# Scaling tokens by two weights: from contiguous 4 MB groups to 128 consecutive tokens in each partition

## The chip, the cores and the metric

The kernel runs on one core of one Trainium2 chip; the other cores run nothing. The metric is the device time of one execution in microseconds. Three executions of the kernel before took 239.26, 242.16 and 251.51 us; their median, 242.16 us, is the time before.

## The reference

The input x has 16 x 1024 tokens of 512 float32 values. Each token has k = 2 expert weights, and the output holds the token once for each weight, multiplied by it. The expert indices are an input, but the result doesn't use them.

```python
batch, seq, hidden, n_experts = 16, 1024, 512, 8          # k = 2
x_expanded = x[:, :, np.newaxis, :].repeat(k, axis=2)
weights = expert_weights[..., np.newaxis]
return (x_expanded * weights).astype(np.float32)          # [16, 1024, 2, 512]
```

So 33.5 MB of x and 0.13 MB of weights are read and 67.1 MB are written, with one multiplication for each number written.

## The kernel before

The 16,384 tokens are cut into eight groups of 2048 consecutive tokens. A group is one tile of 128 partitions, and a partition holds T = 16 tokens of it. For this the helper `rows(flat, done, T)` takes rows done*128 to (done+T)*128 of a flat array, which are one contiguous block, and gives the first 16 to partition 0, the next 16 to partition 1 and so on. In HBM the row that one partition reads (16 tokens of 2 KB, 32 KB) therefore starts 32 KB behind the one of its neighbour, and the row that it writes (64 KB) starts 64 KB behind.

A slot is a tile of 128 x 64 KB, and there are three slots. The load of a group (L120, issued from ScalarE's queue) puts the 32 KB of x into the upper half of the slot. The products are then written from the bottom of the slot upwards, over x that has already been used: VectorE does tokens 0 to 7, 8 to 11, 12 to 13 and 14 in four instructions (L136), and ScalarE does the two products of token 15 in two (L153). SyncE's queue then stores the 64 KB rows (L178). In the first and the last group the first eight tokens are stored by themselves (L174) as soon as their product is done, so these groups have two stores of half the size. The load of group i + 2 is issued behind the last products of group i, from ScalarE's queue, and waits until the store that empties its slot has landed. All instructions stand in the order in which the program writes them.

The weights: a partition of a group needs the 32 weights of its 16 tokens, and the whole tile `w_tile` holds 128 partitions x 8 groups x 32 weights. In HBM the weights of one group's partition are only 128 bytes in a row. The kernel therefore loads them as 128 rows of 1 KB (`weights_in`, L68, from SyncE's queue), in which partition q has the weights of 128 consecutive tokens, and sorts them on the chip (`weights_spread`): eight transposes on TensorE (L84) against an identity that GpSimd writes (L55 and L56), two copies on VectorE (L89), eight transposes back (L95) and a last copy into `w_tile` (L100). The order at the start is: load of the weights, loads of groups 0, 1 and 2, sorting, and then the loop over the groups.

Of the kernel before, what the change touches and what calls it, by code (L numbers as in the profile page):

```python
# [1 line left out]

# [4 lines left out]


@with_exitstack
def kernel(  # L10
    ctx: ExitStack,
    tc: tile.TileContext,
    x: bass.AP,
    expert_indices: bass.AP,
    expert_weights: bass.AP,
    out: bass.AP,
):
    nc = tc.nc

    batch, seq, hidden = x.shape  # L20
    k = expert_weights.shape[-1]
    P = nc.NUM_PARTITIONS
    ntok = batch * seq
    assert ntok % P == 0

    f32 = mybir.dt.float32
    row = k * hidden


    groups = [16] * 8  # L30
    assert sum(groups) * P == ntok
    TX = max(groups)

    xf = x.rearrange("b s h -> (b s) h")
    of = out.rearrange("b s k h -> (b s) (k h)")
    wf = expert_weights.rearrange("b s k -> (b s) k")

    w_pool = ctx.enter_context(tc.tile_pool(name="w_pool", bufs=1))
    slots = ctx.enter_context(tc.tile_pool(name="slots", bufs=3))
    raw_pool = ctx.enter_context(tc.tile_pool(name="raw_pool", bufs=1))  # L40
    psum = ctx.enter_context(
        tc.tile_pool(name="psum", bufs=2, space=bass.MemoryType.PSUM)
    )

    w_tile = w_pool.tile([P, sum(groups) * k], f32)

    def rows(flat, done, T):
        return flat[done * P : (done + T) * P, :].rearrange("(p a) n -> p (a n)", a=T)

    B = 8
    M = P // B
    ident = w_pool.tile([P, P], f32)
    nc.gpsimd.memset(ident, 0.0)  # L55
    nc.gpsimd.affine_select(  # L56
        out=ident,
        in_=ident,
        compare_op=mybir.AluOpType.not_equal,
        fill=1.0,  # L60
        base=0,
        pattern=[[-1, P]],
        channel_multiplier=1,
    )

    def weights_in(head, G, T):
        raw_tile = raw_pool.tile([G * M, B * T * k], f32, name=f"raw{T}_tile")
        nc.sync.dma_start(  # L68
            out=raw_tile,
            in_=wf[head * P : (head + G * T) * P, :].rearrange(  # L70
                "(q a) n -> q (a n)", a=B * T
            ),
        )
        return raw_tile

    def weights_spread(raw_tile, head, G, T):
        n = T * k
        col_tile = raw_pool.tile([n, G * P], f32, name=f"col{T}_tile")
        cols = col_tile.rearrange("c (q r) -> c q r", r=B)
        step = 4  # L80
        for r0 in range(0, B, step):
            up_tile = psum.tile([n, step, G * M], f32)
            for r in range(step):
                nc.tensor.transpose(  # L84
                    up_tile[:, r, :],
                    raw_tile[:, (r0 + r) * n : (r0 + r + 1) * n],
                    ident[: G * M, : G * M],
                )
            nc.vector.tensor_copy(  # L89
                out=cols[:, :, r0 : r0 + step],  # L90
                in_=up_tile.rearrange("c r q -> c q r"),
            )
        down_tile = psum.tile([P, G * n], f32)
        for g in range(G):
            nc.tensor.transpose(  # L95
                down_tile[:, g * n : (g + 1) * n],
                col_tile[:, g * P : (g + 1) * P],
                ident[:n, :n],
            )
        nc.vector.tensor_copy(  # L100
            out=w_tile[:, head * k : (head + G * T) * k], in_=down_tile
        )

    ctx.enter_context(tc.manual_schedule())

    starts = [sum(groups[:i]) for i in range(len(groups))]
    loaded = []

    def load(i):
        if i >= len(groups):
            return
        T = groups[i]
        slot_tile = slots.tile([P, TX * row], f32)
        loaded.append(slot_tile)
        src = rows(xf, starts[i], T)
        at = T * (row - hidden)
        nc.scalar.dma_start(out=slot_tile[:, at : at + T * hidden], in_=src)  # L120


    def ranges(T):
        lo, out = 0, []
        while lo < T - 1:
            hi = lo + 1
            while (hi + 1) * k <= T * (k - 1) + lo and hi < T - 1:
                hi += 1
            out.append((lo, hi))
            lo = hi  # L130
        return out

    def products(slot_tile, T, lo, hi, w_at):
        m = hi - lo
        at = T * (row - hidden) + lo * hidden
        nc.vector.tensor_tensor(  # L136
            out=slot_tile[:, lo * row : hi * row].rearrange(
                "p (t k h) -> p t k h", t=m, k=k
            ),
            in0=slot_tile[:, at : at + m * hidden]  # L140
            .rearrange("p (t h) -> p t h", t=m)
            .unsqueeze(2)
            .to_broadcast([P, m, k, hidden]),
            in1=w_tile[:, w_at + lo * k : w_at + hi * k]
            .rearrange("p (t k) -> p t k", t=m)
            .unsqueeze(3)
            .to_broadcast([P, m, k, hidden]),
            op=mybir.AluOpType.mult,
        )

    def last(slot_tile, T, w_at):
        for c in range(T * k - k, T * k):
            nc.scalar.mul(  # L153
                out=slot_tile[:, c * hidden : (c + 1) * hidden],
                in_=slot_tile[:, T * row - hidden : T * row],
                mul=w_tile[:, w_at + c : w_at + c + 1],
            )

    raw_tile = weights_in(0, 8, 16)
    load(0)  # L160
    load(1)
    load(2)
    weights_spread(raw_tile, 0, 8, 16)

    for i, T in enumerate(groups):
        slot_tile = loaded[i]
        outr = rows(of, starts[i], T)
        w_at = starts[i] * k
        done = 0
        for lo, hi in ranges(T):  # L170
            products(slot_tile, T, lo, hi, w_at)
            if i in (0, len(groups) - 1) and done == 0:
                done = hi
                nc.sync.dma_start(  # L174
                    out=outr[:, : done * row], in_=slot_tile[:, : done * row]
                )
        last(slot_tile, T, w_at)
        nc.sync.dma_start(  # L178
            out=outr[:, done * row :], in_=slot_tile[:, done * row : T * row]
        )  # L180
        if i:
            load(i + 2)

# [1 line left out]
_INS = ['x', 'expert_indices', 'expert_weights']  # L185
_OUTS = [((16, 1024, 2, 512), 'float32')]


# [23 lines left out]
```

## Time and profile before

| | before |
|---|---|
| median of three runs | 242.16 us (239.26 to 251.51) |
| the profiled execution's own time | 239.3 us |
| its span, from the first to the last instruction | 237.5 us |
| bytes moved | 100.80 MB, of which 33.69 MB read and 67.11 MB written |
| mean rate over the span | 424 GB/s |
| busy: VectorE | 134.7 us (57%) |
| busy: ScalarE | 12.8 us (5%) |
| busy: TensorE | 2.9 us (1%) |
| DMA packets | 2736 |

A single execution is profiled; its own time is longer than the span by 1.8 us, which lie outside the first and the last recorded instruction. It is close to the fastest of the three runs. The DMA share is the mean over the core's 16 DMA engines, and packets are counted when they end, so that a short stretch can show more or less than was moved in it. Queue q1 is the one that SyncE issues on (stores and weights), q10 that of ScalarE (loads of x).

### The profile page before, as it was taken

The page shows a single profiled execution, that of the slowest core. Times are in us where ns is not written, and L with a number is a line of the kernel's source. Part 1 is how long each engine was busy: PE and PEld are TensorE (multiplying, and loading weights), DVE is VectorE, ACT ScalarE, POOL GpSimd, SP SyncE. Part 2 cuts the span into 40 slices and gives each one's busy share as a digit, 9 for nine tenths or more (in the row PEclk, how much of TensorE's full clock was granted, in tenths as well). Part 3 has the DMA queues.
Part 4 walks back from the last instruction along what each step waited for, and adds up shares of the span by engine and source line. Part 5 has one row for each costly group of instructions (what it writes and reads, how often), then busy time and mean ns, then how long its engine had stood idle before and what let it go on. Part 6 is the DMA issues. An engine that isn't in the chain of part 4 may idle for free.

```text
span 237.5 us, 184 instructions
## 1 busy us (share of the span) xinstructions
PE 2.9 (1%) x16; PEld 1.9 (1%) x16; DVE 134.7 (57%) x35; ACT 12.8 (5%) x17; POOL 0.7 (0%) x6
## 2 busy tenths in 40 slices
PE   0400000000000000000000000000000000000000
PEld 0300000000000000000000000000000000000000
DVE  0289999999600089900998009970199602995000
ACT  0020020110200000020001100020000200002000
POOL 1000000000000000000000000000000000000000
DMA  7999999999899899899799898998998989989996
GB/s 284 444 441 441 353 441 441 436 447 441 375 419 530 353 441 530 353 441 530 337 458 430 370 524 353 441 530 353 441 530 348 447 386 453 486 353 441 441 441 265
DMA packets 2736, 100.80 MB, mean 424 GB/s; under 512 B 304, under 2 KB 432, under 8 KB 432
## 3 DMA queue, kind: packets, MB, share of 16 engines
q1 hardware_dynamic: 1584, 67.24, 65.5%
q10 hardware_dynamic: 1152, 33.55, 33.2%
HBM read 33.69 MB, written 67.11 MB: 424 GB/s over the span
## 4 chain that ended last, share of the span: by engine, by line
DMA 61%; DVE 28%; ACT 2%; issue 0%; DVEq 0%; ACTq 0%
DMA slot_tile<-in_x_dram 33%; DMA out_dram<-slot_tile 29%; DVE slot_tile L136 28%; ACT slot_tile L153 2%; DVEq L136 0%; ACTq L120 0%
## 5 line engine op out<-in xcount | busy, mean ns | idle before, releaser
L136 DVE TENSOR_TENSOR slot_tile<-slot_tile,w_tile 128x8192 f32<-128x8192 f32 (+3 forms) x32 | 132.9, 4158 | 71.6 <-DMA slot_tile<-in_x_dram 70.7
L153 ACT ACTIVATE slot_tile<-slot_tile,w_tile 128x512 f32<-128x512 f32 x16 | 11.5, 721 | 192.5 <-DVE slot_tile L136 192.3
L89 DVE COPY col_tile<-up_tile 32x512 f32<-32x512 f32 x2 | 1.4, 678 | 9.6 <-PE up_tile L84 9.6
L153 ACT ACT_TABLE_LOAD x1 | 1.3, 1283 | 13.2 <-DMA slot_tile<-in_x_dram 13.2
L84 PE MATMUL up_tile<-ident,raw_tile 128*32 128x128 f32 x8 | 1.9, 411 | 8.4 <-DMA raw_tile<-in_expert_weights_dram 8.4
L84 PEld LDWEIGHTS up_tile<-ident,raw_tile 128*32 128x32 f32 x8 | 1.0, 135 | 8.8 <-issue 8.4
L100 DVE COPY w_tile<-down_tile 128x256 f32<-128x256 f32 x1 | 0.4, 424 | 1.1 <-PE down_tile L95 1.1
L95 PE MATMUL down_tile<-ident,col_tile 32*128 32x32 f32 x8 | 1.1, 292 | 0.8 <-DVE col_tile L89 0.8
L95 PEld LDWEIGHTS down_tile<-ident,col_tile 32*128 32x128 f32 x8 | 0.9, 214 | 1.3 <-DVE col_tile L89 1.3
L56 POOL TENSOR_SCALAR_AFFINE_SELECT ident<-ident 128x128 f32<-128x128 f32 x1 | 0.3, 292 | 0.1
L55 POOL MEMSET ident<- 128x128 f32 x1 | 0.2, 204 | 0.3 <-POOLq L196 0.3
L196 POOL MEMSET const-bfloat16-1.0<- 128x1 bf16 x1 | 0.1, 101 | 0.0
L196 POOL MEMSET const-uint8-127<- 128x1 uint8 x1 | 0.1, 101 | 0.0
L196 POOL MEMSET const-float32-0.0<- 128x1 f32 x1 | 0.1, 98 | 0.2 <-issue 0.2
L196 POOL MEMSET const-float32-1.0<- 128x1 f32 x1 | 0.1, 98 | 0.0
## 6 DMA issues: line engine op xcount, KB each, us to landing
slot_tile<-in_x_dram ACTq DMA_DIRECT2D x8, 4096.0 KB, 32.6
out_dram<-slot_tile SPq DMA_DIRECT2D x4, 4096.0 KB, 19.5
raw_tile<-in_expert_weights_dram SPq DMA_DIRECT2D x1, 128.0 KB, 7.5
out_dram<-slot_tile SPq DMA_DIRECT2D x6, 35.9
```

The lines of the kernel that those rows point to most:

```text
L55: nc.gpsimd.memset(ident, 0.0)
L56: nc.gpsimd.affine_select(out=ident, in_=ident, compare_op=mybir.AluOpType.not_equal, fill=1.0, base=0, pattern=[[-1, P]], channel_multipl ...
L84: nc.tensor.transpose(up_tile[:, r, :], raw_tile[:, (r0 + r) * n : (r0 + r + 1) * n], ident[: G * M, : G * M],)
L89: nc.vector.tensor_copy(out=cols[:, :, r0 : r0 + step], in_=up_tile.rearrange("c r q -> c q r"),)
L95: nc.tensor.transpose(down_tile[:, g * n : (g + 1) * n], col_tile[:, g * P : (g + 1) * P], ident[:n, :n],)
L100: nc.vector.tensor_copy(out=w_tile[:, head * k : (head + G * T) * k], in_=down_tile)
L136: nc.vector.tensor_tensor(out=slot_tile[:, lo * row : hi * row].rearrange("p (t k h) -> p t k h", t=m, k=k), in0=slot_tile[:, at : at + m ...
L153: nc.scalar.mul(out=slot_tile[:, c * hidden : (c + 1) * hidden], in_=slot_tile[:, T * row - hidden : T * row], mul=w_tile[:, w_at + c : w_ ...
L196: nc = _bacc.Bacc("TRN2", target_bir_lowering=False, num_devices=1)
```

## The change

The helper `rows` no longer takes a contiguous block. It gives each partition 128 consecutive tokens of the whole array, and a group is 16 of these tokens in each partition: group 0 has tokens 0 to 15 of every partition's 128, group 1 tokens 16 to 31, and so on. Rows are as long as before (32 KB read, 64 KB written), but the start of one partition's row now lies 256 KB behind that of its neighbour in x, and 512 KB behind in the output. With this the weights of a partition are 128 consecutive pairs, 1 KB, for all groups together, so that one load of 1 KB rows fills `w_tile` as it is used. The identity, the transposes, the copies and the two pools for them go. The loop, the products, the slots and the order of the loads and stores stay.

```diff
-    raw_pool = ctx.enter_context(tc.tile_pool(name="raw_pool", bufs=1))
-    psum = ctx.enter_context(
-        tc.tile_pool(name="psum", bufs=2, space=bass.MemoryType.PSUM)
-    )
...
     def rows(flat, done, T):
-        return flat[done * P : (done + T) * P, :].rearrange("(p a) n -> p (a n)", a=T)
...
-    ident = w_pool.tile([P, P], f32)
-    nc.gpsimd.memset(ident, 0.0)
-    nc.gpsimd.affine_select(
...
-    def weights_in(head, G, T):
...
-    def weights_spread(raw_tile, head, G, T):
...
+        return flat.rearrange("(p a) n -> p a n", p=P)[:, done : done + T, :].rearrange(
+            "p a n -> p (a n)"
         )
...
-    raw_tile = weights_in(0, 8, 16)
-    load(0)
-    load(1)
-    load(2)
-    weights_spread(raw_tile, 0, 8, 16)
+    nc.sync.dma_start(out=w_tile, in_=rows(wf, 0, ntok // P))
+    for i in range(3):
+        load(i)
```

More of the change, by code (lines that the diff above doesn't have):

```diff
@@ L39 @@
     slots = ctx.enter_context(tc.tile_pool(name="slots", bufs=3))
-    raw_pool = ctx.enter_context(tc.tile_pool(name="raw_pool", bufs=1))
-    psum = ctx.enter_context(
-        tc.tile_pool(name="psum", bufs=2, space=bass.MemoryType.PSUM)
-    )
     w_tile = w_pool.tile([P, sum(groups) * k], f32)
     def rows(flat, done, T):
-        return flat[done * P : (done + T) * P, :].rearrange("(p a) n -> p (a n)", a=T)
-    B = 8
-    M = P // B
-    ident = w_pool.tile([P, P], f32)
-    nc.gpsimd.memset(ident, 0.0)
-    nc.gpsimd.affine_select(
[L57 to L64, printed above, removed]
-    def weights_in(head, G, T):
[L67 to L74, printed above, removed]
-    def weights_spread(raw_tile, head, G, T):
[L77 to L101, printed above, removed]
+        return flat.rearrange("(p a) n -> p a n", p=P)[:, done : done + T, :].rearrange(
+            "p a n -> p (a n)"
         )
```

## The prediction

> **What bounds the kernel now.** I read the page's table of engines first, then the DMA rows, then the rate in stretches, then the start in order of time, and last the chain. The first lines of the page:
>
> ```profile
> PE 2.9 (1%) x16; PEld 1.9 (1%) x16; DVE 134.7 (57%) x35; ACT 12.8 (5%) x17; POOL 0.7 (0%) x6
> ...
> DMA  7999999999899899899799898998998989989996
> GB/s 284 444 441 441 353 441 441 436 447 441 375 419 530 353 441 530 353 441 530 337 458 430 370 524 353 441 530 353 441 530 348 447 386 453 486 353 441 441 441 265
> DMA packets 2736, 100.80 MB, mean 424 GB/s; under 512 B 304, under 2 KB 432, under 8 KB 432
> ...
> q1 hardware_dynamic: 1584, 67.24, 65.5%
> q10 hardware_dynamic: 1152, 33.55, 33.2%
> ```
>
> No compute engine is near full: VectorE, the busiest, works 57% of the span. The DMA row is at 8 or 9 tenths in every slice but three. The two queues' packets take 65.5 + 33.2 = 98.7% of what 16 DMA engines have in the span, so the DMA engines stand idle for 1.3% of 237.5 us, 3.1 us in all. The single slices swing between 337 and 530 GB/s because packets of 32 and 64 KB are counted when they end; longer stretches are steadier. Two answers by stretch (columns: the stretch, its length, busy time and count of PE, PEld, DVE, ACT and POOL, the TensorE clock, the DMA share, GB/s):
>
> ```profile
> 0.00:13.00 13.00, 2.92 (x16) 1.93 (x16) 1.78 (x3) 0.00 (x0) 0.70 (x6) 1.00 0.92 373
> 13.00:22.00 9.00, 0.00 (x0) 0.00 (x0) 8.76 (x2) 1.28 (x1) 0.00 (x0) 1.00 0.94 408
> 22.00:49.00 27.00, 0.00 (x0) 0.00 (x0) 26.83 (x8) 2.89 (x4) 0.00 (x0) 1.00 1.02 427
> 49.00:201.00 152.00, 0.00 (x0) 0.00 (x0) 81.40 (x21) 7.21 (x10) 0.00 (x0) 1.00 1.00 435
> ```
>
> ```profile
> 3.00:12.00 9.00, 2.83 (x16) 1.93 (x16) 1.36 (x2) 0.00 (x0) 0.00 (x0) 1.00 0.96 413
> 48.00:80.00 32.00, 0.00 (x0) 0.00 (x0) 15.13 (x4) 1.54 (x3) 0.00 (x0) 1.00 1.01 436
> ...
> 200.00:209.00 9.00, 0.00 (x0) 0.00 (x0) 8.69 (x1) 0.00 (x0) 0.00 (x0) 1.00 0.81 350
> 209.00:236.00 27.00, 0.00 (x0) 0.00 (x0) 7.95 (x3) 1.44 (x2) 0.00 (x0) 1.00 0.99 427
> ```
>
> From 49 to 201 us, when loads and stores run together, the DMA engines are full (share 1.00) and move 435 GB/s. What idle time there is lies at the start (8% of 13 us is 1.0 us, 6% of the next 9 us is 0.5 us) and near the end (19% of the 9 us from 200 is 1.7 us), together 3.2 us, as the queues' shares said. The last hole has a cause that the chain of waits shows:
>
> ```profile
> 167.53 32.62 DMA slot_tile<-in_x_dram
> ...
> 200.28 8.70 DVE slot_tile L136
> ```
>
> The last load lands at about 200.2 us, and until its first product is done 8.70 us later only the rest of the store before it is left to move. So the kernel is a full stream of packets with 3 us of holes; its time is bytes divided by the rate of a packet, plus these holes.
>
> **The change part by part.** *The sorting of the weights goes.* It is 16 matmuls with their weight loads, three VectorE copies and two GpSimd instructions. The start in order of time (start, length, engine, line):
>
> ```profile
> 0.74 0.37 SPq L68 DMA_DIRECT2D raw_tile<-in_expert_weights_dram  x1
> ...
> 8.40 1.86 PE L84 MATMUL up_tile<-ident,raw_tile 128*32 128x128 f32 x8 [8.40 <-DMA raw_tile<-in_expert_weights_dram]
> 9.45 0.68 DVE L89 COPY col_tile<-up_tile 32x512 f32<-32x512 f32 x1 [9.45 <-PE up_tile L84]
> ...
> 12.12 0.42 DVE L100 COPY w_tile<-down_tile 128x256 f32<-128x256 f32 x1 [1.15 <-PE down_tile L95]
> 13.18 1.28 ACT L153 ACT_TABLE_LOAD   x1 [13.18 <-DMA slot_tile<-in_x_dram]
> 13.21 8.69 DVE L136 TENSOR_TENSOR slot_tile<-slot_tile,w_tile 128x8192 f32<-128x8192 f32 x1 [0.66 <-DMA slot_tile<-in_x_dram]
> ```
>
> The weights are in place at 12.12 + 0.42 = 12.54 us. The first product begins at 13.21 us, and what released it is the load of group 0, which lands at 13.1 us. So the sorting lies wholly under that load, 0.66 us short of it, and its removal is worth 0 on the path. The 1.78 us of VectorE copies and 2.92 us of TensorE lie in the same stretch; nothing waits for them. What becomes late next is nothing: the product still waits for group 0.
>
> *The load of the weights* has the same shape as before, 128 rows of 1 KB from the same contiguous 128 KB, issued first on SyncE's queue, at 0.74 us. It only has another target. It lands about 7.5 us after its issue:
>
> ```profile
> raw_tile<-in_expert_weights_dram SPq DMA_DIRECT2D x1, 128.0 KB, 7.5
> ```
>
> ```profile
> 21.93 0.34 SPq L174 DMA_DIRECT2D out_dram<-slot_tile  x1
> ```
>
> So `w_tile` will be ready at about 8.3 us, with 4.9 us to spare against group 0. If that cover went, the first product would be late by the excess; behind it on VectorE stand all products, and behind those the first store at 21.93 us. It would take a landing at 18 us, 10 us after the one seen, to cost 4.9 us. Cost: 0, with 0 at both ends.
>
> *Order and queues.* The listing of the changed program has the same ten stores behind one weight load on SyncE's queue, the same eight loads between the same products on ScalarE's, and the same 32 products on VectorE. No queue gains a wait. The GpSimd instructions that go (0.7 us, with constants that stay) have nobody behind them.
>
> *The pitch of the rows.* All 100.80 MB move in packets of the same length: 1024 of 32 KB for the loads, 768 of 64 KB and 512 of 32 KB for the stores, 128 of 1 KB for the weights, and small ones. What changes is where they lie: the streams that the 16 DMA engines run side by side start 256 KB (reads) and 512 KB (writes) apart for each partition instead of 32 and 64 KB, so eight times as far. The trace of before shows no such pitch, and its cost is the whole question, since the packets fill 98.7% of the span. The nearest rows are those of one kind alone. From 3 to 12 us only loads run, at 32 KB: 413 GB/s at a share of 0.96, so 430 at full share. From 209 to 236 us only stores run, at 64 KB: 427 / 0.99 = 431. One doubling of the pitch (and the change from reading to writing) costs nothing to be seen, which gives the end at 0 cost. For the other end there is no row of a long pitch; the furthest that these same transfers have been seen to slow is the slowest of the three runs, 251.51 us against the profiled execution's 239.3, so +12.2 us, which is 5% of the packets' time. An end below nothing: the best long stretch, 48 to 80 us, had 436 GB/s. At that rate 100.80 MB take 231.2 us; with the 3.1 us of holes, which nothing here removes, 234.3, that is 3.2 us under the span. So the pitch costs between -3.2 and +12.2 us.
>
> I take a third of the upper end, +4.1 us. This is a choice: the row at zero is the nearest, but it stands for one doubling of the pitch, and three are made here, in both directions. It is nearer to zero than to the slow run, as the only row that does speak of pitch asks.
>
> The Trainium skill speaks against this change, in "DMA: Bandwidth & Descriptors", section "Latency and other measured facts": copies of 128 rows of 16 KiB between HBM tensors fell to 207 GB/s a direction where the rows' pitch was 512 KiB and to 164 at 2 MiB, while a padded pitch gave 214. By an estimate from that page the stores' packets (65.5% of the span, 155.6 us) would take 214/207 as long, 5.3 us more, so 244.6 us; with the loads at the same rate it would be 7.9 us and 247.2. No run here has shown it yet.
>
> **The sum.** 239.3 (the profiled execution) + 0 (sorting) + 0 (weights' load) + 0 (order) + 4.1 (pitch) = 243.4 us. The profiled execution is 2.9 us faster than the median of the runs shown, so this is 1.7% over the former and 0.5% over the latter. A difference under 2% (4.8 us) is about what can't be told from no change in this kernel.
>
> **The rivals.**
>
> *The pitch costs over 2%.* Mechanism: the 16 DMA engines take rows of equal length side by side, in step; if starts that are a large power of two apart meet in the same part of the memory, each packet waits for others. It decides from 4.8 us, which is a packet rate of 435 x 234.4 / 239.2 = 426 GB/s or less in the stretch from 49 to 201 us. For it: nothing in the span could hide a slower packet, as the share is 1.00 there. Against it: the pitch of before is a power of two as well, and loads alone and stores alone reach the same rate with it. Its price lies between 4.8 and the 12.2 us of the upper end; the middle, 8.5, gives 247.8 us. The Trainium skill's row above is a rule of this kind.
>
> *The new pitch is better.* Streams that lie further apart may disturb each other less, when loads and stores mix. For it: the mixed stretch is 435 at share 1.00, and single stretches differ by some GB/s. Against it: loads alone, stores alone and the mixture all give 430 to 436 at full share, which looks like the DMA engines' own limit and leaves nothing for the memory to give. Price: up to -3.2, so 236.1 us.
>
> *The change does more than it says at the start*, that is, the path begins with the sorting after all and the product starts once the weights are there, at 8.3 us. That would be worth up to 13.21 - 8.3 = 4.9 us, so 234.4 us. Against it stands the row at 13.21 with its releaser: the load of group 0 is needed whatever the weights do. And an earlier product would still meet a DMA that is 94 to 102% busy from 13 to 49 us.
>
> **How the numbers follow.** The forecast (within 2%, 243.4 us, pitch costs little) gets 0.50. The slow pitch gets 0.40, since the resource it strikes is full in every stretch and has no cover. The better pitch gets 0.08 and the gain at the start 0.02. Of these last 0.10, some 0.06 lie over 2% faster: against a median of runs of 242.16, 236.1 is 2.5% faster, against 239.3 it is 1.3%. So faster 0.06, same 0.54, slower 0.40. The range goes from 236.1, the end of the better pitch, to 251.5, the upper end of the pitch's cost; beyond it I leave 0.15 to the slow side, where a pitch that does alias could cost more than any of the three runs shows, and 0.05 to the fast.
>
> **What would show each step right or wrong.** The sorting: the first product begins at 13.1 to 13.3 us and is still released by the load of group 0, and PE has no instructions. The weights: the load lands near 7.5 us. The order: stores issued first at 21.9 us. The pitch: 2736 packets, 100.80 MB, both as now, and a rate of 428 GB/s or so (435 x 234.4 / 238.5) from 49 to 201 us at a DMA share of 1.00; 426 or less with a longer share of both queues would be the slow rival, and 435 no cost at all. Loads alone at the start (413 GB/s from 3 to 12 us) and stores alone at the end (427 from 209 to 236 us, moved to wherever the last stage lies) would tell which pitch costs: 256 KB or 512 KB. I am wrong if the stream slows strongly, or if the time falls below 236 us, which would mean that a packet can be faster than any stretch of before shows.

## The result and the profile after

The kernel after takes 248.13 us (median of six executions, 246.67 to 248.98); the six of the kernel before beside it have a median of 240.77 us. The ratio after to before is **1.034, with a 95% interval of 1.028 to 1.040**: slower by over 2%. Of the kernel before this ratio takes the four executions from 239.26 to 242.16 us; its other two, 247.24 and 251.51 us, and most of its executions beside the later runs lie as high as those of after, all of which took 246.67 us or more.

The page of after, first the DMA rows and the queues:

```profile
DVE 132.9 (54%) x32; ACT 12.8 (5%) x17; POOL 0.2 (0%) x4
...
DMA  7999999999999989989998999999999998979990
...
DMA packets 2736, 100.80 MB, mean 408 GB/s; under 512 B 304, under 2 KB 432, under 8 KB 432
...
q1 hardware_dynamic: 1584, 67.24, 63.7%
q10 hardware_dynamic: 1152, 33.55, 33.5%
```

The same packets and bytes, in a span of 247.2 us instead of 237.5. The queues' packets now take 63.7 + 33.5 = 97.2% of it: 240.3 us where before they took 234.4, so **5.9 us more in the packets**. The rest of the span, in which a DMA engine stands idle, went from 3.1 to 6.9 us: **3.8 us more in holes**. Together these are the 9.7 us between the two spans. By the starts and lengths of the packets nearly all of the added idle time is the engines' waiting for each other behind the last load (0.5 us on the mean) and at the end of the last store (3.6 us).

By stretch (columns: stretch, length, busy time and count of DVE, ACT and POOL, the TensorE clock, the DMA share, GB/s):

```profile
3.00:12.00 9.00, 0.00 (x0) 0.00 (x0) 0.00 (x0) 1.00 0.98 421
49.00:201.00 152.00, 81.00 (x20) 7.21 (x10) 0.00 (x0) 1.00 1.01 420
...
212.00:222.00 10.00, 9.46 (x2) 0.00 (x0) 0.00 (x0) 1.00 0.91 393
231.00:246.00 15.00, 0.00 (x0) 0.00 (x0) 0.00 (x0) 1.00 0.72 310
```

Loads alone still run at 421 / 0.98 = 430 GB/s at full share, stores alone at the end at 310 / 0.72 = 431, both as before. Only the mixture is slower: 420 GB/s at a share of 1.01, where before had 435 at 1.00. And the last stretch has a share of 0.72: most engines are done while some still work.

The start in order of time, and the chain around the last load:

```profile
0.73 0.37 SPq L103 DMA_DIRECT2D w_tile<-in_expert_weights_dram  x1
13.53 50.04 DVE L80 TENSOR_TENSOR slot_tile<-slot_tile,w_tile 128x8192 f32<-128x8192 f32 x12 [13.53 <-DMA slot_tile<-in_x_dram]
```

```profile
173.57 38.80 DMA slot_tile<-in_x_dram
...
212.50 8.70 DVE slot_tile L80
```

The first product begins at 13.53 us, behind the load of group 0 as before. The last load is issued 6.0 us later than before (173.57 against 167.53) and takes 38.80 us instead of 32.62, so it lands 12.2 us later.

Each load and store is shared by the 16 DMA engines, and the trace has the moment at which each of them is done with its share. Worked out from these moments and from the records of the packets (us of the span; a load packet is 32 KB, a store packet 64 KB; the means are over packets that start between 72 and 190 us, which is all mixture):

```
                              before            after
last load, first engine       199.7             201.1
last load, last engine        200.2             212.4
  spread                        0.4              11.3
last store, spread              0.4               4.4
load packet, median / mean    1.213 / 1.213     1.213 / 1.291
  longer than 1.25 us          0%                18%
store packet, mean            2.418             2.460
```

In before, the 16 engines move in step: every packet takes the same time and all engines finish within half a microsecond. In after, most packets are as short as before, but some are long, and they push single engines back. The first engine is done with the last load only 1.4 us later than before; the product waits for the last one, which is 12.2 us later. Behind that load the rest takes 34.8 us (247.2 - 212.4) instead of 37.3, because less of the store ahead of it is left. 12.2 - 2.5 gives the 9.7 us.

### The profile page after: what moved, and what is told of

Its sections match the earlier page's. It is cut to its first block, busy times and chain, and to the rows that moved or that the text cites. A ratio compares the mean times of both kernels' runs of the same rounds, so it can differ in the third digit from the quotient of the medians.

```text
span 247.2 us, 141 instructions
## 1 busy us (share of the span) xinstructions
DVE 132.9 (54%) x32; ACT 12.8 (5%) x17; POOL 0.2 (0%) x4
## 3 DMA queue, kind: packets, MB, share of 16 engines
q1 hardware_dynamic: 1584, 67.24, 63.7%
q10 hardware_dynamic: 1152, 33.55, 33.5%
## 4 chain that ended last, share of the span: by engine, by line
DMA 64%; DVE 27%; ACT 2%; issue 0%; DVEq 0%
DMA slot_tile<-in_x_dram 36%; DMA out_dram<-slot_tile 29%; DVE slot_tile L80 27%; ACT slot_tile L97 2%; DVEq L80 0%
```

## The experiments

Times are the median of the executions with the lowest and the highest; kernels of one group below ran on one chip, beside the kernel before.

**The sorting alone.** The kernel before, with the weights loaded straight into `w_tile` (`rows` in the new line is the helper of after; x and the output keep the old one):

```diff
-    raw_tile = weights_in(0, 8, 16)
+    nc.sync.dma_start(out=w_tile, in_=rows(wf, 0, ntok // P))
...
-    weights_spread(raw_tile, 0, 8, 16)
```

> The kernel before with its contiguous groups (rows 32 and 64 KB apart), but w_tile is filled by the one load of the kernel after and the sorting is gone; the products so use weights of other tokens, with the same instructions. Theory that the sorting was hidden: first product at 13.1 to 13.3 us behind the load of group 0, time as before, 239 to 241 us, ratio 1.00. Theory that the direct load of the weights is part of the loss: about 248 us.

Four executions: 239.09, 239.30, 246.32 and 247.95 us; the kernel before on that chip had 239.22 to 251.51. The profiled execution took 239.09 us, with a span of 237.3. Its timeline, and its rate in the mixture:

```profile
13.25 13.15 DVE L83 TENSOR_TENSOR slot_tile<-slot_tile,w_tile 128x8192 f32<-128x8192 f32 x2 [13.25 <-DMA slot_tile<-in_x_dram]
...
21.97 0.34 SPq L119 DMA_DIRECT2D out_dram<-slot_tile  x1
```

```profile
49.00:201.00 152.00, 81.48 (x21) 7.21 (x10) 0.00 (x0) 1.00 1.00 435
```

The first product begins at 13.25 us against 13.21, and the span differs by 0.2 us. In this execution the sorting was hidden and the direct load costs nothing: what is left as the cause of the loss is the pitch. The two executions at 246.32 and 247.95 us lie where the kernel before has some too.

**Reads and writes, each alone.** One of the two layouts stays as in before (`near` is the old `rows`):

```diff
     e2_far_reads:
-        outr = rows(of, starts[i], T)
+        outr = near(of, starts[i], T)
     e3_far_writes:
-        src = rows(xf, starts[i], T)
+        src = near(xf, starts[i], T)
```

> The kernel after, but the output rows lie 64 KB apart as in the kernel before (x rows stay 256 KB apart), so the products are stored to the places of other tokens. In the kernel after the loads' packets rose by 5% in sum (66 us of 1262 over 16 engines) and the 64 KB stores' by 1.5% (28 of 1857). Theory R, the reads' pitch does it: about 246 to 248 us, ratio 1.025 to 1.035. Theory W, the stores' pitch does it and the loads are only hit by it: 239 to 241 us, ratio 1.00. Theory that both pitches have a part: in between, 242 to 245 us.

> The other half: x rows 32 KB apart as in the kernel before, output rows 512 KB apart as after; again the products are stored to the places of other tokens. Theory R: 239 to 241 us. Theory W: 246 to 248 us. Both: 242 to 245 us, and the two halves' losses together make the 8 us or so of the whole change.

Far reads: 248.04 us (244.33 to 249.19), ratio 1.028 (1.017 to 1.039). Far writes: 245.91 us (244.34 to 248.56), ratio 1.023 (1.017 to 1.029). Neither verdict is clear of 2%, and none of the theories holds as it stood: each half alone brings most of the loss, and the halves don't add up. The profiles differ in kind, though. With far reads the packets took 235.4 us an engine in sum (before 234.5, after 240.2) and their means hardly moved, 1.220 and 2.431 us; but from about 110 us on one single engine fell back, up to 9.6 us behind the next of the other fifteen, and the loads and stores waited for it. With far writes the load packets rose to 1.268 us and the packets' sum to 238.0 us, and the engines, too, ended up to 11.3 us apart. So there are two things, an engine that lags and packets that are long, and on two queues they are mixed up.

**A pitch that is no power of two.** Seven groups share blocks of 112 tokens a partition, the eighth is contiguous; rows lie 224 and 448 KB apart:

```diff
+    BLOCKS = [112, 16]          # consecutive tokens of a partition in a block
...
+        return flat[at * P : (at + A) * P, :].rearrange("(p a) n -> p a n", a=A)[
+            :, done - at : done - at + T, :
+        ].rearrange("p a n -> p (a n)")
```

> Groups 0 to 6 take 16 tokens each of 112 consecutive tokens of a partition, and group 7 the last 2048 tokens as one block. Rows then lie 224 and 448 KB apart, nearly as far as after but no power of two; two loads fill w_tile. Theory that starts a large power of two apart meet in the memory: time as before, 239 to 241 us, all 16 engines land their shares of a load within 0.5 us as before. Theory that mere distance costs (many far regions open at once): nearly as slow as after, 246 to 248 us, with a spread of several us between the engines.

247.13 us (242.12 to 251.51), with the engines up to 13.1 us apart. Taken by itself this speaks for distance and against the power of two. Its profiled execution took 249.25 us, far above its best, so this trace doesn't show what the layout can do; the question was put again below, where it came out the other way.

**Shorter pitches.** The same helper with BLOCKS = [64, 64] and [32] * 4:

> Two blocks of 8192 tokens, in each of which a partition holds 64 consecutive tokens: x rows 128 KB apart, output rows 256 KB, half of the pitch after; two loads of 512-byte rows fill w_tile. Pitch of seven rows (224 and 448 KB) had run at 247 us with engines up to 13 us apart, so a power of two isn't needed for the loss. Theory that the distance of the rows costs step by step: 243 to 245 us, with a smaller spread between the engines' landings than after's 11 us. Theory that any layout in which a group isn't one contiguous block loses the engines' step: 246 to 248 us, like after. Theory that only the largest pitches lose it: 239 to 241 us.

> Four blocks, 32 consecutive tokens a partition: x rows 64 KB apart, output rows 128 KB, twice that of before. Distance step by step: 240 to 242 us. Any layout that isn't contiguous: 246 to 248 us. Only the largest pitches: 239 to 241 us.

128 and 256 KB: 243.23 us (240.23 to 245.88). 64 and 128 KB: 243.08 us (239.50 to 249.27). Four executions each, widely scattered, while the kernel before beside them had a median of 248.40 (239.37 to 248.87). This can't decide between the theories. What can be read is the lowest time of each layout: 239.09 to 239.50 with rows up to 64 and 128 KB apart, 240.23 with 128 and 256, 242.12 with 224 and 448, 246.67 with 256 and 512. With more pitch the executions in step seem to go away; how often each layout has one can't be told from so few.

The profiled execution with 64 and 128 KB, one of the long ones at 246.63 us, shows something else. Its rate from 49 to 201 us:

```profile
49.00:201.00 152.00, 80.57 (x20) 7.21 (x10) 0.00 (x0) 1.00 1.00 422
```

Here 16% of the load packets in the mixture are longer than 1.25 us, their mean is 1.285 us and that of the store packets 2.470, and the engines end a load up to 8.4 us apart. Those are nearly the numbers of after, at a quarter of its pitch, in a kernel that took 239.50 and 239.53 us in two other executions. On two queues the long packets and the lagging engines are therefore no mark of the far pitch, and the profile of after alone doesn't show what that pitch costs.

**One queue.** The loads go to SyncE's queue, behind the stores:

```diff
-        nc.scalar.dma_start(out=slot_tile[:, at : at + T * hidden], in_=src)
+        nc.sync.dma_start(out=slot_tile[:, at : at + T * hidden], in_=src)
```

> The kernel after, with the loads of x issued from SyncE's queue too, behind the store that the program has before them; so on one DMA engine a load's and a store's packets no longer take turns. In after, loads alone (before 22 us) and stores alone (at the end) had packets as short as before's, and only the mixture had long ones (load packets 1.24 to 1.40 us on the mean against 1.213). Theory that the mixture is where an engine falls behind: 236 to 240 us, engines within 1 us of each other. Theory that the far rows are slow in themselves: 246 us or more.

> The same single queue for the kernel before, with its contiguous groups. Theory of the mixture: as the run with far rows, 236 to 240 us; and its runs lie closer together than those of before, which go from 239 to 251 us. In both, the last load goes ahead of the last but one store, so that the hole near the end (1.7 us before, 5.6 us after) shrinks. Rival, the turns of loads and stores are needed to keep the engines busy: slower than 242 us, with the DMA share under 0.95 in the middle stretch.

Far rows: 249.75 us (249.20 to 250.79). Near rows: 242.02 us (240.56 to 242.87). The scatter is gone, and the two layouts stand 7.7 us apart. The theory that the mixture on one engine is the whole cause falls with the first, where the engines are still up to 5.0 us apart. In the second, the engines stay within 1.2 us of each other in all loads and stores of the profile. The near rows fit neither expectation: 242.02 us is over the 236 to 240 of the one, and the share of 1.01 is far from the 0.95 of the other. From 49 to 201 us, far rows first:

```profile
49.00:201.00 152.00, 80.97 (x20) 7.21 (x10) 0.00 (x0) 1.00 1.00 414
```

```profile
49.00:201.00 152.00, 0.00 (x0) 0.00 (x0) 82.91 (x21) 7.21 (x10) 0.00 (x0) 1.00 1.01 434
```

Near rows keep the 434 GB/s of before; far rows have 414 at the same share. There was no hole of 1.7 us near the end to win (the next section has why), and near rows on one queue are no faster than before's best, 239.37 us on that chip. They are steadier: on that chip before had 248.40 us as its median.

**Which pitch, on one queue.** The edits of the halves, of the seven-row pitch and of the shortest pitch, each with the loads on SyncE's queue. In both halves the products are stored to the places of other tokens.

> One queue for loads and stores, x rows 256 KB apart as after, output rows 64 KB apart as before (products stored to the places of other tokens). On one queue the two layouts stand clear of each other: near rows 240.6 to 242.9 us, far rows 249.2 to 250.8, with load packets of 1.22 to 1.23 us against 1.35 to 1.37 in the middle stages. Theory that the stores' pitch disturbs what moves beside them: 241 to 243 us. Theory that the loads' own pitch makes them long: 247 to 250 us. Both have a part: 244 to 247 us.

> One queue, x rows 32 KB apart as before, output rows 512 KB apart as after. Stores' pitch: 247 to 250 us, load packets at 1.3 us or more in the middle stages although their own rows are near. Loads' pitch: 241 to 243 us. Both: 244 to 247 us, and the two excesses over 242 add up to about 8 us.

> One queue, rows 224 and 448 KB apart (seven rows), the last group contiguous. Power of two matters after all: 241 to 243 us. Distance alone: 248 to 250 us, as the far rows.

> One queue, rows 64 and 128 KB apart, four loads of 256-byte rows fill w_tile, no sorting. The pitch costs step by step: 243 to 246 us. Only the large pitches cost: 240 to 243 us, which would be a kernel without the sorting that is as fast and as steady as the near rows on one queue.

```
one queue, rows apart (reads, writes)     us, median (lowest to highest)   load packet   longer than 1.25 us   store packet
 32,  64 KB  (near)                       242.02 (240.56 to 242.87)        1.224          7%                   2.418
 64, 128 KB                               243.44 (242.68 to 244.14)        1.242         11%                   2.418
224, 448 KB                               243.28 (242.75 to 243.69)        1.224          4%                   2.418
256,  64 KB  (far reads)                  243.16 (243.13 to 243.51)        1.229          6%                   2.418
 32, 512 KB  (far writes)                 251.28 (250.97 to 251.49)        1.376         45%                   2.477
256, 512 KB  (far)                        249.75 (249.20 to 250.79)        1.362         39%                   2.449
```

The near and the far row ran on one chip, the four others together on another, so a microsecond between the two groups isn't to be read. What stands out is eight times that. From 49 to 201 us, far reads first, then far writes, then seven rows:

```profile
49.00:201.00 152.00, 81.37 (x20) 7.21 (x10) 0.00 (x0) 1.00 1.01 434
```

```profile
49.00:201.00 152.00, 81.22 (x20) 7.21 (x10) 0.00 (x0) 1.00 1.00 409
```

```profile
49.00:201.00 152.00, 81.54 (x20) 7.21 (x10) 0.00 (x0) 1.00 1.01 437
```

Far reads keep 434 GB/s; far writes alone bring the rate down to 409; and a writes' pitch of 448 KB, seven eighths of 512, keeps 437. So on one queue **it is the stores' rows at 512 KB that cost, and the cost doesn't grow step by step with the distance**: 448 KB takes the same time as 128 (243.28 and 243.44 us on one chip), and 512 KB takes 8 us more. The 243.44 us by itself lies in the range given for a cost step by step; beside 448 KB it doesn't speak for one. Whether it is the power of two, or a limit of the distance between 448 and 512, no run tells: stores at another large power of two (256 KB, on one queue) and at a pitch over 512 KB weren't run. That rows a power of two apart meet in the same part of the memory remains an inference.

The packets that grow most are the loads': in the run with far writes the x rows lie as near as before, and yet 45% of the load packets in the mixture are long. The trace tells where they stand. On one queue loads and stores take turns (with far writes a store runs from 83.1 to 104.9 us, the load behind it from 102.7 to 116.1). The 128 packets of each load and store can so be cut, in order of their starts, into eighths of 16 packets, as many as there are engines. The mean time over the usual 1.213 and 2.418 us, in ns, for the last five loads and the six whole stores:

```
                     eighth    1     2     3     4     5     6     7     8
far writes, loads            177   130   168    25     0    40   417   321
far writes, stores             0     0     0     0     0     0     2   474
far reads, loads               0    12     1     0     0     0     2   135
far reads, stores              0     0     0     0     0     0     0     0
```

The far rows cost at the turns from stores to loads and from loads to stores; between the turns the packets are nearly as short as before. That fits with loads alone at the start and stores alone at the end running at full rate in the kernel after. It isn't only that loads and stores of different engines run side by side: 98 of the 228 long load packets between 72 and 190 us had no store packet beside them at any time. What goes on at a turn isn't shown.

All this is shown for one queue. On two, as in the change itself, far reads alone took no less time than far writes (248.04 and 245.91 us), and the kernel before itself often takes 247 us and more. How much of the 8 us there is the stores' pitch, and how much the lost step, isn't separated.

## Why the prediction was right or wrong

*The bound* was right: a full stream of packets, whose cost goes straight into the time. *The sorting, the weights' load and the order* at 0 were right: the kernel without the sorting has the same span to 0.2 us, and in after the first product still waits for group 0. The weights land 7.9 us after their issue (7.5 before):

```profile
w_tile<-in_expert_weights_dram SPq DMA_DIRECT2D x1, 128.0 KB, 7.9
```

*The pitch* was the step that failed. I took +4.1 us, a third of the upper end, because loads alone and stores alone showed nothing; the time rose by 8.8 us over the profiled execution before (248.13 - 239.3). The measured time lies in the range, at the rival "the pitch costs over 2%", which had 247.8 us and a chance of 0.40 against the forecast's 0.50. That 247.8 came so near is partly luck: it is the middle between 2% and the slowest run of before, and that run has near rows, so its 251.51 us says nothing of a pitch. The same run gave the upper end of the range. The row at zero was the wrong one to lean on: after, too, has 430 and 431 GB/s where one kind runs alone, so these stretches can't show the price. The mixture is slower, and the rate there, 420 GB/s, is under the 426 at which I let this rival decide. It isn't the price of the far pitch alone, though, since the profile with 64 and 128 KB on two queues had 422; 409 against 434 on one queue is.

*The holes*, "which nothing here removes", I had left at 3.1 us in every case. They grew to 6.9. I had thought of all packets as a little slower, and so of one rate. In fact the median packet is unchanged, some are much longer, and engines drift apart; waiting for the last engine of a load or store is 3.8 of the 9.7 us. The rival's mechanism, "each packet waits for others", is therefore right only for a part of the packets.

I had also put the holes in the wrong place. The share of 0.81 from 200 to 209 us is no hole: packets are counted when they end, the engines move in step, and three store packets of 2.418 us that end in 9 us make 0.81. The 9 us from 199 have 1.08, those from 201 have 1.07. The store before the last load's product runs until 217.1 us and keeps all engines busy. By the starts and lengths of the packets the idle time of before lies in the first 3 us (2.0 us in all) and after the last packet (1.4 us), and nowhere between.

*Which pitch*: loads alone and stores alone "would tell" which of the two costs, I wrote. They told nothing. On one queue the halves did: 512 KB on the stores 251.3 us, 256 KB on the loads 243.2.

*The Trainium skill's row* on the pitch ("DMA: Bandwidth & Descriptors", section "Latency and other measured facts") was the better guide. Its 214 against 207 GB/s at a pitch of 512 KiB is 3.4%; the ratio measured is 1.034, and far writes on one queue stand at 251.28 / 243.16 = 1.033 to far reads on the same chip and at 251.28 / 242.02 = 1.038 to near rows, by medians from two chips. The row is of another case, copies from HBM to HBM with the pitch on both sides, and on two queues the match is partly luck, since 3.8 of the 9.7 us are holes and not rate. Its estimates in the prediction were 244.6 us for the stores alone and 247.2 with the loads, against the 248.13 measured. In the same row a pitch of 4 MiB, padded by 4 KiB, has the full rate back; the 437 GB/s at seven rows are in line with that.

## What to carry to other kernels

Where a kernel is a full stream of loads and stores, look at the pitch of the rows that its 128 partitions store to: on one queue 512 KB cost 8 us of 240 here, 448 KB nothing that can be told. Judge a layout by the stretch where loads and stores mix, since each alone may run at full rate. And look at when the first and the last DMA engine finish a transfer: a product waits for the last, so one lagging engine is the time of all.

## What the runs showed that was not expected

- One engine of 16 can fall behind by itself: in the profile of far reads on two queues fifteen engines finished the last store but three within 2.3 us of the first and one 11.3 us after it, while the packets' sum rose by only 0.9 us an engine (235.4 against 234.5).
- On two queues the kernel before is in step in some executions (8 of 27 on one chip at 239.2 to 239.8 us) and not in the others (241.4 to 251.5). On one queue it took 240.6 to 242.9 us each time, four times, where the two-queue kernel beside it had a median of 248.4. Its median is the lowest of the kernels tried on that chip; its best is 1.2 us behind the best of before there (240.56 against 239.37). What makes an execution lose its step on two queues wasn't found.
- A store's pitch lengthens the loads that take turns with it: on one queue load packets of 1.376 us instead of 1.224 with the same x rows.
